# Attention scores on 128 rows everywhere, and a rebalanced weave of routing and expert projection

## The chip, the cores and the metric

The kernel is one program on one core of one Trainium2 chip. The metric is the device time of one execution in microseconds; it was run three times, and the median is 1797.61. One further execution was profiled; it took 1796.13, and every row below comes from it. Times in rows count from the start of its span of 1794.4 us.

## The reference, cut to what matters

256 tokens of width 1024 pass through three blocks in fp32. What the change touches is the scores of the four attentions and the expert layer at the end:

```
# block 1: 'fox' attention (16 heads of 64), then 'nsa' attention (16 heads, 4 key groups)
logits = einsum('bqhd,bkhd->bhqk', q, k) * scale        # fox adds a per-head bias c[q] - c[k]; causal; softmax
# block 2: 8 stick-breaking heads, 8 dilated heads, then a dense feed-forward layer
z  = einsum('bhqd,bhkd->bhqk', q_blk, k) * scale
# block 3: 8 causal heads beside a pooling mixer, then the experts:
q = (h @ w_q).reshape(T, 8, 2, 128);  s = einsum('thpd,hpnd->thpn', q, sub_keys)
sv, si = top_k(s, 16)                                    # 16 of 128 keys in each half
cv, ci = top_k(sv[:, :, 0, :, None] + sv[:, :, 1, None, :], 16)   # 16 of 256 pairs
g = softmax(cv);  expert = si0 * 128 + si1               # 16384 experts
a = gelu(einsum('cd,chkd->chk', x, u_tab[expert]))
y = einsum('chk,chkd->cd', g * a, v_tab[expert])
```

The kernel doesn't gather experts. It computes gelu(x u) for all 16384 of them, multiplies it with a dense matrix of gates (zero where an expert wasn't chosen), and multiplies the product with all of v.

## The kernel before, in words

**Arithmetic.** An fp32 product is made of three products of fp32r halves: `mm3` (L450 to L452) multiplies high by high, low by high and high by low. Every weight tile of 128 x 1024 comes by DMA from the SP queue, ACT copies its high part (`whi`, L241), and DVE subtracts for its low part (`wlo`, L242). For the tiles in the set `W.on_pool` GpSimd (POOL) makes the low part; the set ends ten tiles into the expert matrix u. Three pairs of parts are held, and parts are made two tiles ahead of their use.

**Attention scores.** Head dimension is 64, and two heads lie in the two halves of the 128 partitions. `stack` (L514) builds for a head pair a tile `str` that holds high and low part of one operand in the two halves, a tile `stc` that holds the high part of the other operand twice, and a tile `stl` with its low part, 64 rows for each head. `mm_stack` (L530) then needs two matmuls: one over 128 rows (L533) and one over 64 rows (L534). The second block of 128 queries goes this way. The first block of queries is a plain fp32 matmul over 64 rows (L539 in `attn_scores`, L1114 for the stick-breaking heads), which runs as two passes. The nsa attention has six matmuls for a head, three over 128 rows (L915) and three over 64 (L916).

In each attention stage the heads run as a side of `weave`: the main side is a projection that yields after every step, and after each yield the side's account gets `rate`, and the side runs on until the costs that it yields have used that up:

```
    for _ in main:
        for i, (g, rate) in enumerate(sides):
            acc[i] += rate
            while acc[i] > 0:
                acc[i] -= next(g, 1e9) or 1
    for g, _ in sides:
        drain(g)
```

So rates and yielded costs set the order in which instructions are written; a scheduler then fixes each engine's order at build time. [...]

**The experts.** `peer` first projects the queries (span 925 to 982 us) and finds the top 16 keys on DVE as the heads arrive. Then comes a weave whose main side is the projection by u: 128 tiles of 24 matmuls of 256 columns, made in pairs, with 9 yields to a pair, 576 in all; after a pair ACT applies gelu (L1501). Its only side is `combine`, with the rate `R_PEER`: first `routing` (the last top-16 searches, the softmax of the gates whose exponential is L1453, one-hot expansions of the chosen indices, transposes), which yields 52.5 in all, and then 64 steps of four tokens. A step makes one-hot matrices on DVE (`onehots`, five operations of 512 elements, L1526, L1527 and L1530, cost `OHCOST` = 2.1), multiplies them on PE to a 128 x 128 matrix of gates for a token (12 matmuls, L1549), and multiplies or copies the gates into the activations (L1559 on DVE, L1562 on ACT), cost `EVCOST` = 0.9. Activations of tiles that come later than a step are multiplied with the gates then (L1505). What is left of the side when the main side ends is drained alone. After that come 16 transposes of the residual (L1611) and 16 small ones for a gate vector (L1617), and the projection by v (L1589, 128 tiles, span about 1437 to 1785), for which each tile of the activations is split in two (L1577, L1578).

## Time and profile before

| | |
|---|---|
| three runs, us | 1796.85, 1797.61, 1797.82 (median 1797.61) |
| profiled execution, us | 1796.13 (span 1794.4) |
| PE (TensorE) busy | 1730.8 us, 96% of the span |
| DVE (VectorE) busy | 1291.0 us, 72% |
| ACT (ScalarE) busy | 948.1 us, 53% |
| POOL (GpSimd) busy | 194.9 us, 11% |
| stages in the span, us | fox 0 to 157, nsa to 376, block 2 attention to 527, its feed-forward to 753, block 3 attention to 925, expert queries to 982, u with the weave to 1397, rest of the steps to 1437, v to 1785 |

Rows of a timeline give the start and the duration of an instruction, or of several alike that follow each other (x2), and in brackets how long the engine had been idle and what ended it. PE's matmuls are pipelined, so that the duration of one is longer than the distance to the next: the cost on PE is read from one start to the next. "64*128 64x256" is a matmul over 64 rows with 256 columns. Rows of windows give a stretch, its length, and for PE, its weight loads, DVE, ACT and POOL the busy time and the instructions (x), then TensorE's granted clock as a share of the full 2.4 GHz, the DMA share and GB/s.

### The profile page before, as it was taken

How to read it: one execution, taken by the hardware profiler on the slowest of the kernel's cores; microseconds unless marked ns; L12 is line 12 of the kernel's file. 1: busy time of each engine (PE TensorE's matmuls, PEld its weight loads, DVE VectorE, ACT ScalarE, POOL GpSimd, SP SyncE). 2: the span in 40 equal slices, each digit the busy share in tenths (PEclk: the TensorE clock that was granted, in tenths of full speed). 3: DMA queues.
4: the chain of work that ended last, by engine and by line, in shares of the span. 5: the costliest groups of instructions: out<-in, count | busy, mean ns of one | idle time of the engine just before them, and what ended most of it. 6: DMA issues, size and time to landing. Idle time of an engine off the chain costs nothing.

```text
span 1794.4 us, 31693 instructions
## 1 busy us (share of the span) xinstructions
PE 1730.8 (96%) x12108; PEld 1564.8 (87%) x12108; DVE 1291.0 (72%) x2682; ACT 948.1 (53%) x1783; POOL 194.9 (11%) x194
## 2 busy tenths in 40 slices
PE   8999999999999999999999899999999699999997
PEld 6889897777888999889999799999999588888886
DVE  5777756678767676777667957778889955656565
ACT  5655554555755555566644445544444155555554
POOL 1000124414021000110027300000000000000000
PEclk9999999999999999999999899999999699999999
DMA  6434532248625777534545455545545155655563
GB/s 228 131 120 140 176 110 88 70 168 286 204 95 178 260 259 256 182 123 142 187 156 165 141 188 165 165 154 165 165 154 164 45 179 190 198 190 198 190 197 117
DMA packets 84087, 300.07 MB, mean 167 GB/s; under 512 B 10144, under 2 KB 11040, under 8 KB 83680
## 3 DMA queue, kind: packets, MB, share of 16 engines
q1 hardware_dynamic: 83360, 296.39, 50.1%
q8 instruction: 95, 1.56, 0.4%
q10 hardware_dynamic: 576, 1.66, 0.3%
q14 instruction: 56, 0.46, 0.1%
HBM read 296.04 MB, written 1.05 MB: 166 GB/s over the span
## 4 chain that ended last, share of the span: by engine, by line
PE 81%; DVE 8%; DMA 6%; issue 2%; ACT 2%; POOL 1%; POOLq 0%; SPq 0%; DVEq 0%; ACTq 0%
PE s L1589 10%; PE t L1589 10%; PE pj L450 9%; PE pj L451 9%; PE pj L452 9%; DMA wraw<-in_ada 4%; PE s L450 3%; PE t L450 3%; PE t L452 3%; PE s L451 3%; PE t L451 3%; PE s L452 3%; PE o L1549 2%; PE o L583 2%; DVE wlo L242 1%
## 5 line engine op out<-in xcount | busy, mean ns | idle before, releaser
L242 DVE TENSOR_TENSOR wlo<-wraw,whi 128x1024 fp32r<-128x1024 f32 x480 | 592.2, 1237 | 209.3 <-ACT whi L241 207.7
L241 ACT CAST whi<-wraw 128x1024 fp32r<-128x1024 f32 x504 | 528.3, 1050 | 392.9 <-PE pj L451 131.5
L450 PE MATMUL pj<-hxh,whi 128*128 128x256 f32 x1456 | 423.2, 291 | 4.6 <-ACT vN L1062 1.2
L451 PE MATMUL pj<-hxl,whi 128*128 128x256 f32 x1456 | 413.9, 285 | 0.6 <-DVE hxl L1158 0.4
L452 PE MATMUL pj<-hxh,wlo 128*128 128x256 f32 x1456 | 413.1, 284 | 1.4 <-DVE wlo L242 0.8
L450 PEld LDWEIGHTS pj<-hxh,whi 128*128 128x128 f32 x1456 | 278.3, 191 | 14.2 <-issue 5.0
L452 PEld LDWEIGHTS pj<-hxh,wlo 128*128 128x128 f32 x1456 | 277.7, 191 | 3.6 <-DVE wlo L242 1.2
L451 PEld LDWEIGHTS pj<-hxl,whi 128*128 128x128 f32 x1456 | 278.0, 191 | 2.7 <-DVE hxl L1158 1.1
L1589 PE MATMUL s<-whi,hxl 128*128 128x512 f32 x512 | 158.2, 390 | 0.0
L1589 PE MATMUL t<-whi,hxl 128*128 128x512 f32 x512 | 157.6, 389 | 0.0
L450 PE MATMUL s<-hxh,whi 128*128 128x256 f32 x456 | 131.5, 288 | 1.2 <-DVE st L560 1.2
L1577 ACT CAST hxl<-a 128x256 fp32r<-128x256 f32 x128 | 52.0, 407 | 150.9 <-PE t L1589 150.9
L452 PE MATMUL s<-hxh,wlo 128*128 128x256 f32 x456 | 129.5, 284 | 0.0
L451 PE MATMUL s<-hxl,whi 128*128 128x256 f32 x456 | 129.4, 284 | 0.0
L450 PE MATMUL t<-hxh,whi 128*128 128x256 f32 x424 | 121.9, 288 | 4.7 <-ACT whi L241 4.7
L452 PE MATMUL t<-hxh,wlo 128*128 128x256 f32 x424 | 120.4, 284 | 4.0 <-DVE wlo L242 4.0
L451 PE MATMUL t<-hxl,whi 128*128 128x256 f32 x424 | 120.3, 284 | 0.0
L1589 PEld LDWEIGHTS s<-whi,hxl 128*128 128x128 f32 x512 | 96.3, 188 | 19.9
L1589 PEld LDWEIGHTS t<-whi,hxl 128*128 128x128 f32 x512 | 96.1, 188 | 20.0
L1578 DVE TENSOR_TENSOR hxl<-a,hxl 128x256 fp32r<-128x256 f32 x128 | 54.4, 425 | 64.0 <-PE t L1589 60.0
L291 DVE SCALAR_TENSOR_TENSOR wraw<-wraw,cb 128x1024 f32<-128x1024 f32 x48 | 60.5, 1263 | 44.1 <-DMA wraw<-in_ada 43.9
L450 PEld LDWEIGHTS s<-hxh,whi 128*128 128x128 f32 x456 | 87.6, 192 | 2.2 <-issue 1.9
(400 smaller groups left out, 3422.4 us busy)
## 6 DMA issues: line engine op xcount, KB each, us to landing
wraw<-in_pu SPq DMA_DIRECT2D x128, 512.0 KB
wraw<-in_pv SPq DMA_DIRECT2D x128, 512.0 KB
wraw<-in_b_ffn SPq DMA_DIRECT2D x66, 512.0 KB
wraw<-in_ada SPq DMA_DIRECT2D x48, 512.0 KB
wraw<-in_b_qk SPq DMA_DIRECT2D x24, 512.0 KB
wraw<-in_fox_qk SPq DMA_DIRECT2D x16, 512.0 KB
wraw<-in_b_o SPq DMA_DIRECT2D x16, 512.0 KB
wraw<-in_b_g SPq DMA_DIRECT2D x16, 512.0 KB
```

The lines of the kernel that those rows point to most:

```text
L241: nc.scalar.copy(hi, r)
L242: (nc.gpsimd if self.np in self.on_pool else nc.vector).tensor_tensor(lo, r, hi.bitcast(F32), op=OP.subtract)
L291: nc.vector.scalar_tensor_tensor(t, t, 1.0, cb, op0=OP.mult, op1=OP.mult, accum_out=modT[:, i:i + 1])
L450: nc.tensor.matmul(o, wh, xh, start=start, stop=False)
L451: nc.tensor.matmul(o, wh, xl, start=False, stop=False)
L452: nc.tensor.matmul(o, wl, xh, start=False, stop=stop)
L583: nc.tensor.matmul(o, v(0), pt[:, 0:256], start=start, stop=False)
L1549: nc.tensor.matmul(p[:, t, :], x[:, w[0], :, w[1]], y[i][:, w[0], :, w[1]], start=i == 0 and t == 0, stop=i == 2, skip_group_check=True)
L1577: nc.scalar.copy(ah, src)
L1578: nc.vector.tensor_tensor(al, src, ah.bitcast(F32), op=OP.subtract)
L1589: nc.tensor.matmul(acc[tb][h], x[:, t], w[:, h * 512:h * 512 + 512], start=n == 0 and i == 0, stop=n == P - 1 and i == 2)
```

## The change

1. **Scores.** `stack` makes the stacked operand for both blocks of queries (256 columns instead of 128), and the low part gets its own zero half: the tiles `low` hold 128 rows, of which POOL clears all once, and DVE fills the half of the head. `mm_stack` then runs both matmuls over 128 rows, and the first block of queries uses it too, so that the plain fp32 matmuls L539 and L1114 are gone. In the nsa attention `kl` becomes two tiles with a zero half, and the three matmuls L916 get 128 rows. To make room, the buffers of `qk` are laid out anew (three become one in block 3; in nsa they go into the space of the keys). The matmuls of a score are now L545 (high) and L546 (low), the bias L556.
2. **Weave of the experts.** `R_PEER` goes from 0.36 to 0.43 and `EVCOST` from 0.9 to 1.0; the costs that `routing` yields sum to 37.0 instead of 52.5.
3. **The exponential** of the gates is issued after the first half of the one-hot expansion, not before it.
4. **`W.on_pool`** ends four tiles into u instead of ten: six low parts go from POOL to DVE.
5. A table of 0 to 127 shares a buffer that was there.

From L560 on a line's number after the change differs by some 3 to 12 (the steps' L1526, L1530, L1549, L1559 become L1529, L1533, L1552, L1562; L1453 becomes L1459).

```diff
-R_PEER, TOK, OHCOST, EVCOST = 0.36, 4, 2.1, 0.9
+R_PEER, TOK, OHCOST, EVCOST = 0.43, 4, 2.1, 1.0
-        W.on_pool = set(range(first_u - 14, first_u + 10))
+        W.on_pool = set(range(first_u - 14, first_u + 4))
+        def lows(n, *shape):
+            r = [ph.tile([P, 2, *shape], F32R, name=f"low{i}") for i in range(n)]
+            for t in r:
+                nc.gpsimd.memset(t.bitcast(F32), 0.0)
+            return r
         def stack(rows, cols):
-            r = ph.tile([P, 2, P], F32R, name="str", bufs=SB[i_blk])
+            if low["of"] != i_blk:
+                low.update(of=i_blk, n=lows(SB[i_blk], S))
+            r = ph.tile([P, 2, S], F32R, name="str", bufs=SB[i_blk])
             c = ph.tile([P, 2, S], F32R, name="stc", bufs=SB[i_blk])
-            cl = ph.tile([P, S], F32R, name="stl", bufs=SB[i_blk])
+            cl = low["n"].pop(0)
+            low["n"].append(cl)
...
-                nc.vector.tensor_tensor(cl[a, :], cols[a], c[a, e, :].bitcast(F32), op=OP.subtract)
+                nc.vector.tensor_tensor(cl[a, e, :], cols[a], c[a, e, :].bitcast(F32), op=OP.subtract)
...
-        def mm_stack(o, st, e, stop, skip=False):
-            r, c, cl = st
-            a = HALF[e]
-            nc.tensor.matmul(o, r[:, e, :], c[:, e, :], start=True, stop=False, skip_group_check=skip)
-            nc.tensor.matmul(o, r[a, e, :], cl[a, :], start=False, stop=stop, skip_group_check=skip)
+        def mm_stack(o, st, e, rows, cols, start, stop, skip=False):
+            r, c, cl = (t[:, e, :] for t in st)
+            r = r[:, rows * P:rows * P + P]
+            nc.tensor.matmul(o, r, cols(c), start=start, stop=False, skip_group_check=skip)
+            nc.tensor.matmul(o, r, cols(cl), start=False, stop=stop, skip_group_check=skip)
-        def attn_scores(qT, kT, bias_mm, bias, st2):
+        def attn_scores(bias_mm, bias, st2, e):
             s = ps.tile([P, 512], F32, name="s")
-            nc.tensor.matmul(s[:, 0:P], qT[:, 0:P], kT[:, 0:P], start=True, stop=bias_mm is None)
...
+            for qb in range(2):
+                n = P + P * qb
+                mm_stack(s[:, qb * S:qb * S + S], st2, e, qb, lambda x: x, True, bias_mm is None)
...
-                kl = ph.tile([P, 2, 2, S], F32R, name="kl", tag="Z")
+                kl = [ph.tile([P, 2, 2, S], F32R, name="kl", tag=t) for t in ("Z", "kl")]
...
-                            nc.tensor.matmul(o, qs[c][hs, e, q0:q0 + P], l, start=False, stop=True)
+                            nc.tensor.matmul(o, qs[c][:, e, q0:q0 + P], l, start=False, stop=True)
...
-                yield 6
+                yield 4
...
-                        yield 1.4
+                        yield 1
...
-                nc.scalar.activation(gv, gv, AF.Exp)
-                yield 1.2
+                yield 0.8
                 for tb in range(2):
                     q = eq[tb]
+                    if tb:
+                        nc.scalar.activation(gv, gv, AF.Exp)
...
-                    yield 2.3
+                    yield 1.6
...
-                    yield 2.8
+                    yield 1.8
```

**A head of the fox attention on PE.** Between projection matmuls (L450 to L452) stood, before, the fp32 matmul of the first query block, its bias, and the two matmuls of the second block with their bias (`c_155`, `sel` are the bias operands):

```order
L452 MATMUL pj<-hxh,wlo 128x256
L539 MATMUL s<-qk 128x128
L541 LDWEIGHTS sel
L541 MATMUL s<-c_155,sel 128x128
L533 MATMUL s<-stc,str 128x256
L534 MATMUL s<-stl,str 128x256
L544 LDWEIGHTS sel
L544 MATMUL s<-c_155,sel 128x256
L450 MATMUL pj<-hxh,whi 128x256
```

Now, at a head of the same stage:

```order
L452 MATMUL pj<-hxh,wlo 128x256
L545 MATMUL s<-stc,str 128x256
L546 MATMUL s<-low_478,str 128x256
L556 LDWEIGHTS sel
L556 MATMUL s<-c_155,sel 128x128
L545 MATMUL s<-stc,str 128x256
L546 MATMUL s<-low_478,str 128x256
L556 LDWEIGHTS sel
L556 MATMUL s<-c_155,sel 128x256
L450 MATMUL pj<-hxh,whi 128x256
```

Two matmuls of 256 columns stand in the place of the fp32 one, and the operand with the low part is a `low` tile. Each head of the block 2 dilated heads and of block 3 has the same four matmuls without bias.

**The routing on DVE and ACT, about six tiles of u into the weave.** On DVE, before, these are rows of the top-16 search in the second half of the tokens; no low part (L242) stands among the search's rows:

```order
L1428 TENSOR_TENSOR ra<-ra 128x8x56
L1386 MAX_INDEX ra<-ra 128x8
L1431 TENSOR_TENSOR ra<-ra 128x8x8
L1382 MAX ra<-ra 128x8 x2
L1383 MAX_INDEX ra<-ra 128x8
```

Now, at the same operations (L1430 and L1433 were L1428 and L1431):

```order
L1430 TENSOR_TENSOR ra<-ra 128x8x56
L1387 MAX ra<-ra 128x8
L1433 TENSOR_TENSOR ra<-ra 128x8x8
L242 TENSOR_TENSOR wlo<-wraw,whi 128x1024
L1388 MAX_INDEX ra<-ra 128x8
L1384 MAX ra<-ra 128x8 x2
```

A low part now stands between two searches. From the search's start to the last multiplication of the routing there are 16 of them on DVE, where 9 were, all of them behind the search. On ACT, before, the exponential (L1453) stood behind the gelus of the third pair of u, a high part ahead of the next pair's gelus:

```order
L1501 ACTIVATE a_10601<-t 128x256 x2
L241 CAST whi<-wraw 128x1024
L1453 ACT_TABLE_LOAD
L1453 ACTIVATE ra<-ra 128x256
L241 CAST whi<-wraw 128x1024
L1501 ACT_TABLE_LOAD
L1501 ACTIVATE a_10601<-pj 128x256 x2
```

Now it (L1459) stands behind the fifth pair's:

```order
L1504 ACTIVATE a_10637<-pj 128x256 x2
L241 CAST whi<-wraw 128x1024 x2
L1504 ACTIVATE a_10637<-s 128x256 x2
L1459 ACT_TABLE_LOAD
L1459 ACTIVATE ra<-ra 128x256
L241 CAST whi<-wraw 128x1024 x2
L1504 ACT_TABLE_LOAD
L1504 ACTIVATE a_10637<-t 128x256 x2
```

It has moved by two pairs of u.

**The end of the weave on PE.** Before, the last row of the last step stands long behind the last projection matmul and directly ahead of the transposes and of the projection by v (L1589):

```order
L1549 MATMUL o<-ohy_17326,ohx 128x128
L1611 MATMUL o<-ident,xT 128x128 x12
L1589 MATMUL s<-whi,hxl 128x512 x2
L1611 MATMUL o<-ident,xT 128x128 x4
L1589 MATMUL s<-wlo,hxl 128x512 x2
```

Now (L1614, L1620 and L1592 were L1611, L1617 and L1589) the last projection matmul stands there:

```order
L450 MATMUL pj<-hxh,whi 128x256
L451 MATMUL pj<-hxl,whi 128x256
L452 MATMUL pj<-hxh,wlo 128x256
L1614 MATMUL o<-ident,xT 128x128 x8
L1620 MATMUL pj<-ident,modT 128x128 x8
L1614 MATMUL o<-ident,xT 128x128 x8
L1592 MATMUL s<-whi,hxl 128x512 x2
```

All 64 steps stand ahead of it; before, 51 did, and 13 stood behind it.

## Rows read from the trace of the kernel before

**Rows 1.** The page: the engines' busy time, share of the span and instructions.

```profile
PE 1730.8 (96%) x12108; PEld 1564.8 (87%) x12108; DVE 1291.0 (72%) x2682; ACT 948.1 (53%) x1783; POOL 194.9 (11%) x194
```

**Rows 2.** The timeline of PE at a head of the fox attention.

```profile
81.46 0.28 PE L452 MATMUL pj<-hxh,wlo 128*128 128x256 f32 x1
81.67 0.48 PE L539 MATMUL s<-qk 64*128 64x128 f32 x2
...
82.13 0.36 PE L533 MATMUL s<-stc,str 128*128 128x256 f32 x1
82.42 0.38 PE L534 MATMUL s<-stl,str 64*128 64x256 f32 x1
82.73 0.28 PE L544 MATMUL s<-c,sel 128*128 128x256 bf16 x1
82.77 0.37 PE L450 MATMUL pj<-hxh,whi 128*128 128x256 f32 x1
```

**Rows 3.** The timeline of PE at a head of the nsa attention.

```profile
322.54 0.28 PE L915 MATMUL s<-k,q 128*128 128x256 f32 x1
322.75 0.39 PE L916 MATMUL s<-kl,q 64*128 64x256 f32 x1
323.06 0.39 PE L915 MATMUL s<-k,q 128*128 128x256 f32 x1
...
324.32 0.39 PE L452 MATMUL pj<-hxh,wlo 128*128 128x256 f32 x1
```

**Rows 4.** The timeline of PE around a dilated head of block 2: the last projection matmul ahead of it and the first behind it.

```profile
497.38 0.28 PE L452 MATMUL pj<-hxh,wlo 128*128 128x256 f32 x1
...
498.63 0.39 PE L450 MATMUL pj<-hxh,whi 128*128 128x256 f32 x1
```

**Rows 5.** The timeline of PE at the start of block 3's heads, where the fp32 matmuls of two heads stand one behind the other.

```profile
787.07 0.49 PE L539 MATMUL s<-qk 64*128 64x128 f32 x4 [0.86 <-DVE qk L626]
787.49 0.39 PE L452 MATMUL pj<-hxh,wlo 128*128 128x256 f32 x1
```

**Rows 6.** Windows (columns as above) within the nsa, the fox, the block 2 and the block 3 attention.

```profile
288.00:302.00 14.00, 14.00 (x81) 10.84 (x81) 10.41 (x56) 10.63 (x39) 5.94 (x12) 1.00 0.01 2
45.00:150.00 105.00, 105.00 (x756) 90.58 (x755) 78.26 (x200) 64.46 (x154) 5.17 (x4) 1.00 0.38 121
430.00:530.00 100.00, 99.37 (x640) 80.42 (x641) 74.30 (x159) 71.23 (x170) 11.76 (x19) 1.00 0.49 160
790.00:825.00 35.00, 34.03 (x222) 27.63 (x222) 28.51 (x82) 22.19 (x59) 2.78 (x3) 1.00 0.32 101
```

**Rows 7.** The instructions of line 523 (the copy into the stacked operand) in the whole span: shortest, median and longest in ns, first and last start.

```profile
L523 ACT CAST str<-qk x40: 281/295/299, 49.0 to 815.7; 64x128 fp32r<-64x128 f32 x40
```

**Rows 8.** Windows of the weave by u: its start with the routing, its last 97 us, and the steps that follow it.

```profile
981.60:1021.20 39.60, 30.98 (x242) 30.48 (x242) 38.62 (x182) 17.90 (x25) 18.57 (x8) 0.87 0.37 120
1300.00:1397.30 97.30, 97.30 (x907) 96.57 (x906) 89.30 (x172) 43.53 (x107) 0.00 (x0) 1.00 0.50 160
1397.30:1437.00 39.70, 25.42 (x189) 18.67 (x187) 37.41 (x88) 5.71 (x12) 0.00 (x0) 0.62 0.09 27
```

**Rows 9.** The timelines of ACT and, below it, of PE where the exponential of the routing stands.

```profile
1011.56 0.42 ACT L1453 ACTIVATE ra<-ra 128x256 f32<-128x256 f32 x1 [9.57 <-DVE ra L1452]
1012.97 0.58 PE L450 MATMUL t<-hxh,whi 128*128 128x256 f32 x1 [4.65 <-ACT whi L241]
1017.73 0.58 PE L452 MATMUL t<-hxh,wlo 128*128 128x256 f32 x1 [3.97 <-DVE wlo L242]
```

**Rows 10.** Timelines of POOL (the first row) and DVE in the routing; the last row groups DVE's low parts from 1011.12 to 1037.6, where the routing ends.

```profile
986.37 2.41 POOL L242 TENSOR_TENSOR wlo<-wraw,whi 128x1024 fp32r<-128x1024 f32 x1 [0.48 <-ACT whi L241]
982.39 0.49 DVE L1382 MAX8 ra<-ra 128x8 f32<-128x128 f32 x2 [0.93 <-ACT ra L1402]
986.62 2.31 DVE L1427 TENSOR_TENSOR ra<-ra 128x128 f32<-128x128 f32 x1
1000.04 0.41 DVE L1427 TENSOR_TENSOR ra<-ra 128x128 f32<-128x128 f32 x1
1001.27 2.19 DVE L1431 TENSOR_TENSOR ra<-ra 128x64 f32<-128x64 f32 x1
L242 DVE TENSOR_TENSOR wlo<-wraw,whi 128x1024 fp32r<-128x1024 f32 x9 | 10.8, 1218 | 0.0
```

**Rows 11.** The timeline of PE at a step late in the weave.

```profile
1331.20 0.28 PE L451 MATMUL t<-hxl,whi 128*128 128x256 f32 x1
1331.32 0.28 PE L452 MATMUL t<-hxh,wlo 128*128 128x256 f32 x1
1331.45 0.86 PE L1549 MATMUL o<-ohy,ohx 128*128 128x128 bf16 x12
1332.12 0.36 PE L450 MATMUL pj<-hxh,whi 128*128 128x256 f32 x1
1332.32 0.28 PE L451 MATMUL pj<-hxl,whi 128*128 128x256 f32 x1
```

**Rows 12.** The timeline of PE in the steps behind the weave: the first of them, one wait from the middle, and the first transposes behind the last.

```profile
1397.19 1.55 PE L1549 MATMUL o<-ohy,ohx 128*128 128x128 bf16 x24
...
1419.73 1.22 PE L1549 MATMUL o<-ohy,ohx 128*128 128x128 bf16 x10 [0.67 <-DVE ohy L1530]
...
1432.34 1.05 PE L1611 MATMUL o<-ident,xT 128*128 128x128 f32 x4
```

More of the change, by code (lines that the diff above doesn't have):

```diff
@@ L525, in stack @@
                 nc.vector.tensor_tensor(r[b, e, :], rows[a], r[a, e, :].bitcast(F32), op=OP.subtract)
-                nc.vector.tensor_tensor(cl[a, :], cols[a], c[a, e, :].bitcast(F32), op=OP.subtract)
+                nc.vector.tensor_tensor(cl[a, e, :], cols[a], c[a, e, :].bitcast(F32), op=OP.subtract)
                 nc.scalar.copy(c[b, e, :], cols[a])
             return r, c, cl
-        def mm_stack(o, st, e, stop, skip=False):
-            r, c, cl = st
-            a = HALF[e]
-            nc.tensor.matmul(o, r[:, e, :], c[:, e, :], start=True, stop=False, skip_group_check=skip)
-            nc.tensor.matmul(o, r[a, e, :], cl[a, :], start=False, stop=stop, skip_group_check=skip)
-        def attn_scores(qT, kT, bias_mm, bias, st2):
-            s = ps.tile([P, 512], F32, name="s")
-            nc.tensor.matmul(s[:, 0:P], qT[:, 0:P], kT[:, 0:P], start=True, stop=bias_mm is None)
-            if bias_mm is not None:
-                nc.tensor.matmul(s[:, 0:P], bias_mm[0], bias_mm[1][:, 0:P], start=False, stop=True)
-            mm_stack(s[:, P:P + S], *st2, bias_mm is None)
-            if bias_mm is not None:
-                nc.tensor.matmul(s[:, P:P + S], bias_mm[0], bias_mm[1], start=False, stop=True)
-            return softmax((s[:, 0:P], s[:, P:P + S]), bias)
+        def mm_stack(o, st, e, rows, cols, start, stop, skip=False):
[4 more added lines that the diff above has]
+        def attn_scores(bias_mm, bias, st2, e):
+            s = ps.tile([P, 512], F32, name="s")
+            for qb in range(2):
+                n = P + P * qb
+                mm_stack(s[:, qb * S:qb * S + S], st2, e, qb, lambda x: x, True, bias_mm is None)
+                if bias_mm is not None:
+                    nc.tensor.matmul(s[:, qb * S:qb * S + n], bias_mm[0], bias_mm[1][:, 0:n], start=False, stop=True)
+            return softmax((s[:, 0:P], s[:, S:2 * S]), bias)
         def softmax(s, bias):
@@ L689, in qk_evac @@
                 nc.vector.tensor_tensor(qk[:, c0 // 2], p, rqk, op=OP.mult)
-                stacks[c0 // 2] = stack(qk[:, c0 // 2, 0, P:], qk[:, c0 // 2, 1, :])
+                stacks[c0 // 2] = stack(qk[:, c0 // 2, 0, :], qk[:, c0 // 2, 1, :])
                 cnt["qk"] = c0 // 2 + 1
@@ L880, in q_evac @@
                 nc.vector.tensor_tensor(x, p, rq[:, None, :].to_broadcast([P, 2, S]), op=OP.mult)
-                qT[c0 // 2] = q = ph.tile([P, 2, S], F32, name="qk", bufs=2)
+                qT[c0 // 2] = q = ks[2][:, c0 // 2 % 2]
                 rope([(q, (slice(None),) * 3)], x, C["ropeC"][:, None, :].to_broadcast([P, 2, S]),
@@ L1069, in qk_evac @@
                 q, k = qk[:, c, 0, :], qk[:, c, 1, :]
-                stacks[c] = stack(k[:, :P], q) if c < 4 else stack(q[:, P:], k)
+                stacks[c] = stack(k, q) if c < 4 else stack(q, k)
                 cnt["qk2"] = c + 1
@@ L1103, in attn @@
                         c = h // 2
[L1104 removed]
                         while cnt.get("qk2", 0) <= c:
                             yield
[L1107 removed]
                         if h < 8:
                             z = ps.tile([P, 512], F32, name="s")
[L1110 to L1115 removed]
+                            for kb, cols_of in enumerate((lambda x: x, lambda x: x[:, None, P:].to_broadcast([P, 2, P]))):
+                                o = kb * S
+                                mm_stack(z[:, o:o + S], stacks[c], h % 2, kb, cols_of, kb == 0, False, True)
                                 nc.tensor.matmul(z[:, o:o + P], sbm[:, 0, :], sbm[:, 1, :], start=False, stop=kb == 1,
@@ L1238, in qk_evac @@
                 nc.scalar.copy(x, p)
-                qk[c] = ph.tile([P, 2, S], F32, name="qk", bufs=3)
+                qk[c] = ph.tile([P, 2, S], F32, name="qk", bufs=1)
                 rope([(qk[c], (slice(None),) * 3)], x, rt[:, 0], rt[:, 1], space)
-                stacks[c] = stack(qk[c][:, 0, P:], qk[c][:, 1, :])
+                stacks[c] = stack(qk[c][:, 0, :], qk[c][:, 1, :])
                 cnt["qk3"] = c + 1
@@ L1358, in peer @@
             nc.scalar.dma_start(sk, A["sk"])
-            iota = ph.tile([P, P], F32, name="iota")
+            iota = take("a", P)
             nc.scalar.dma_start(iota, A["iota"])
```

40 lines of the change are left out of this document (14 added, 26 removed).

## The prediction, made before the changed kernel ran

> **What bounds the kernel now.** I read the page first, then windows of the stages, then PE's timeline at the places that change. PE is busy for 96% of the span [rows 1], in most windows at a granted clock of 1.00, that is 2.4 GHz [rows 6], so time is saved where PE's own work gets shorter, or where it stands still or at a lower clock. The windows show which it is where. In the fox, block 2 and block 3 attentions PE is busy for 105.00 of 105, 99.37 of 100 and 34.03 of 35 us, with DVE at 75 to 81% [rows 6]: work removed from PE there shortens the stage as long as DVE and the softmax behind it keep up. In the weave by u there are two soft spots [rows 8]: its start, where PE is busy for only 30.98 of 39.6 us at a clock of 0.87, and the stretch behind it, 25.42 of 39.70 us at 0.62. There DVE is the busy engine (38.62 and 37.41 us).
>
> **The scores.** The step from one projection matmul to the next is 0.12 us (1331.20 to 1331.32) [rows 11]. A fox head takes 81.58 (0.12 behind the start at 81.46) to 82.77, 1.19 us [rows 2]. Of that a 256-column matmul over 128 rows that is followed by one over 64 rows takes 0.29 (82.13 to 82.42), and the 64-row one 0.31 (82.42 to 82.73), each some 2.5 times the 0.12: what is dear is going from 128 rows to 64 and back. Without that the head is four matmuls of 0.12, two biases of 0.04 (82.73 to 82.77), and some allowance for the change between bf16 and fp32r at each bias, 0.07 as an estimate (behind the bf16 matmuls of a step the next one takes 0.20 and not 0.12, 1332.12 to 1332.32 [rows 11]); 0.70 us, with bounds of 0.60 and 0.88. Saved: 16 heads by 0.49 = 7.8 us. A dilated head or one of block 3 takes 1.13 (497.50 to 498.63) [rows 4] and becomes 0.48: 16 by 0.65 = 10.4. For the 8 stick-breaking heads, with two bias matmuls of the larger kind, I estimate 0.46 each, 3.7. An nsa head is six matmuls in 1.78 (322.54 to 324.32), with 0.21 and 0.31 in turn [rows 3], and becomes 0.72: 16 by 1.06 = 17.0. Gross 38.9 us.
>
> How much is kept depends on the covers. In the fox stage DVE has 78 us of work in 105 [rows 6], so 8 us less PE time still leaves it under 82%; I keep 7 of 7.8 (bounds 5 and 9.5). For blocks 2 and 3 I keep 12 of 14.1 (9 to 15). In nsa the window shows PE 14.00, DVE 10.41, ACT 10.63 and POOL 5.94 of 14 us [rows 6]: in itself room, but with a score's two banks refilled head by head, the chain score, softmax, exponential, POOL's normalization, transposes is nearly as long as PE's work beside it. When a head's scores shrink by 1.06 us, PE will come early to the next transposes and wait. I keep 10 of 17 (5 to 17).
>
> The price is wider stack copies: 40 on ACT, now 0.295 us for 128 columns [rows 7]; 256 columns took ACT 0.42 in the exponential [rows 9], so 0.125 more each, and as many on DVE. That is 5 us on either engine, in stages where ACT is busy for 61 to 71% and DVE for 75 to 81% [rows 6]; I cost it at nothing, and if the cover were gone it would be those 5 us. POOL's clearing stands on an engine with 5 to 12 us of work in these windows. The first query block now waits for the stack, where it waited for `qk` alone (0.86 us once [rows 5]): minus 1. Attention in sum: 7 + 12 + 10 - 1 = 28 us (17 to 40).
>
> Here a rule speaks against the change. In rows 5 four 64-row matmuls of two heads, which lie in different halves of the rows, take only 0.42 us (787.07 to 787.49), so a pair overlapped. The Trainium skill ("TensorE: Matmul & The Clock Gate", section "Why this matters for your kernels") says that small matmuls in distinct row groups run concurrently and that a single one over few rows takes as long as one over all 128. By it a 64-row matmul would cost what a 128-row one does, the gain from rows would be nil, and an overlap would be thrown away. The trace agrees with the overlap at that one place; it doesn't agree with equal cost where rows alternate (0.31 against 0.12 [rows 2, 11]). The Trainium skill's page "TensorEngine Tiling (Array Packing)", section "Key Properties", says that a change of the tiling mode drains TensorE, which fits that 0.31.
>
> **The weave by u.** First the stretch behind it. The steps that were left run from 1397.19 to 1432.34, 35.1 us, 24 matmuls to begin with for two steps [rows 12]; 11 more follow, 13 in all. In the weave a step costs PE 0.67 + 0.08 = 0.745 us (1331.45 to 1332.12, and then 0.20 to the next one instead of 0.12) [rows 11]. The account shows why they fit now: routing took 52.5 / 0.36 = 146 of the 576 yields, and 430 yields x 0.36 / 3.0 gives 51 steps; now 37 / 0.43 = 86 and 490 x 0.43 / 3.1 = 68, more than the 64 there are. So 35.1 go and 13 x 0.745 = 9.7 come. The 16 transposes that stood between those steps now wait behind the weave: minus 1. The other transposes, the copies and the split before the projection by v stay as they are.
>
> Second its start. ACT sits 9.57 us at the exponential for DVE's routing (till 1011.56), and the high part that PE needs stands behind it; PE then waits 4.65 us for that and 3.97 for a low part [rows 9], with matmuls at 1.2 GHz after it: 39.6 - 30.98 = 8.6 idle and about 1.5 of slow matmuls, 10 us. Now the exponential stands two pairs later, 11.5 us of PE. DVE's routing took from 982.39 to 1037.57, 55.2 us, with 9 low parts of 1.14 in it, 10.3 [rows 10]. It also had operations that took 2.31 and 2.19 us beside low parts on POOL (986.37), where the same operation took 0.41 at 1000.04; three such, 5.7 us. They go, since POOL's last low part now ends before 986. That leaves 39.2 us, and with 16 low parts (18.3) it ends at 982.4 + 57.5 = 1039.9. PE, undisturbed, comes to the routing's transposes behind 19.6 tiles of 24 x 0.12 = 2.88 us, at 1038.1. So PE waits about 2 us there (0 to 8) in place of 10: 8 won.
>
> Third, the price: DVE. In the last 97.3 us it is busy for 89.30 [rows 8]. A step took 3.0 / 0.36 = 8.33 yields, 1.85 tiles, 1.85 x 2.88 + 0.745 = 6.08 us of PE; so 16 steps stand there, with 5.58 us of DVE each, 2.1 of it low parts. Now a step comes every 7.2 yields, 1.61 tiles: PE 5.38, DVE 1.61 x 1.14 + 3.47 = 5.30. DVE is at 98.6% late in the weave; it was 92%. I take 3 us of waits (0 to 15).
>
> In sum: 35.1 - 9.7 - 1 + 8 - 3 = 29 us (17 to 32).
>
> **Sum.** 28 + 29 = 57. The profiled execution took 1796.13 us, so 1739; the median of the runs lies 1.5 above it, so **1741 us**.
>
> **Rivals.** *The softmax chain eats the scores' gain.* For: nsa's tight chain. Against: the full PE and the free DVE of the others [rows 6]. With 2 us kept in nsa and 10 elsewhere: 1796 - 12 - 29 + 1.5 = 1757. *DVE becomes the bound late in the weave.* For: 98.6%. If it is late by 0.5 us in each of the last 30 steps, 15 us go: about 1755. *A padded matmul gains nothing* (the rule above): only the weave's 29 are left, 1769; rows 2 and 3 speak against it. *Slower.* If DVE's demand passes PE's 5.38 us, PE waits in each step, as it did behind the weave (0.67 us ahead of ten matmuls [rows 12], clock 0.62 [rows 8]), and its clock falls. At 1.2 GHz a step is 38.6 matmuls of some 0.21 and 1.1, 9.3 us; then DVE catches up and the clock returns. At half and half 7.4, 2.0 us more than 5.38; over 30 steps 60, more than the 57 won: about 1801. It decides from 5.38 us of DVE per step, 0.08 from my estimate; against it, PE showed no wait worth naming in that window with DVE at 92%.
>
> **Numbers.** My forecast 0.65, with a range of its own of 1726 to 1756; softmax chain 0.14; DVE late 0.11; nothing from rows 0.05; slower 0.04, and 0.01 for a cancellation near zero. The range of 1725 to 1766 leaves out the last three and tails of the first. 0.2% (3.6 us) is about what a measurement of this kernel can tell from no change: faster 0.95, same 0.01, slower 0.04.
>
> **What would show it.** Right: fox heads near 0.7 us and nsa heads near 0.72 on PE; no 64-row score matmul left; attention stages ending some 6, 16 and 28 us earlier by fox, nsa and block 3; one wait of a few us near tile 20 of u; the projection by v starting within 6 us of the last projection matmul by u. Wrong: waits of PE for `pn` or for ACT in nsa, one-hot matmuls that wait for `ohy` in the last 100 us of the weave, or a clock below 1.00 there.

## The result, and the profile after

The changed kernel takes 1725.9 us (median of four runs, 1724.79 to 1728.64), against 1797.23 before in the same comparison: a ratio of 0.9615, interval 0.9598 to 0.9631. That is 71 us less, where 57 were forecast; the time lies just inside the range, at its lower end. The profiled execution took 1728.64 us, 67.5 less than the profiled one before. PE's line of the page, against [rows 1]:

```profile
PE 1680.3 (97%) x12108; PEld 1545.8 (90%) x12108; DVE 1294.4 (75%) x2691; ACT 959.2 (56%) x1813; POOL 185.7 (11%) x198
```

PE's busy time fell by 50.5 us and its idle time by 17, so the gain is mostly work or slow matmuls taken from PE, not waits. The stages show where. In each I took the start of the same projection matmul (the L450 with the same number in PE's order) in both traces:

| place | before | after | gain so far |
|---|---|---|---|
| end of the fox stage (L450 no. 240) | 166.2 | 158.8 | 7.4 |
| end of nsa (no. 520) | 391.4 | 362.8 | 28.6 |
| start of the feed-forward of block 2 (no. 720) | 548.3 | 513.0 | 35.3 |
| behind it (no. 1040) | 723.3 | 690.5 | 32.7 |
| behind block 3's attention (no. 1440) | 930.8 | 894.2 | 36.6 |
| last projection by u (no. 2575) | 1396.8 | 1365.1 | 31.8 |
| last matmul of the projection by v | 1784.9 | 1717.5 | 67.5 |

The heads have shrunk as computed. A fox head on PE, against [rows 2]:

```profile
87.08 0.28 PE L452 MATMUL pj<-hxh,wlo 128*128 128x256 f32 x1
87.20 0.28 PE L545 MATMUL s<-stc,str 128*128 128x256 f32 x1
87.31 0.28 PE L546 MATMUL s<-low,str 128*128 128x256 f32 x1
...
87.80 0.28 PE L556 MATMUL s<-c,sel 128*128 128x256 bf16 x1
87.84 0.36 PE L450 MATMUL pj<-hxh,whi 128*128 128x256 f32 x1
```

From 87.20 to 87.84 it is 0.64 us; it was 1.19. The second matmul now starts 0.11 behind the first, where 0.29 stood. An nsa head, against [rows 3]:

```profile
235.31 0.28 PE L923 MATMUL s<-k,q 128*128 128x256 f32 x1
235.42 0.28 PE L924 MATMUL s<-kl,q 128*128 128x256 f32 x1
...
236.01 0.40 PE L832 MATMUL o<-whi,zh 128*128 128x256 f32 x1
```

It takes 0.70 (235.31 to 236.01) instead of 1.78.

Windows of the kernel before: the nsa stage, and 40 us in it where its heads begin.

```profile
157.00:376.00 219.00, 210.88 (x1343) 181.74 (x1342) 148.20 (x406) 118.19 (x268) 59.50 (x79) 0.97 0.34 112
225.00:265.00 40.00, 40.00 (x194) 35.69 (x194) 21.22 (x70) 20.23 (x47) 7.21 (x11) 0.91 0.35 121
```

The same of the kernel after, and below them the start of the weave by u and 100 us late in it, against [rows 8] (busy us of PE, PE's loads, DVE, ACT, POOL; then the clock):

```profile
150.00:348.00 198.00, 188.49 (x1344) 171.40 (x1342) 150.09 (x406) 117.09 (x267) 59.67 (x80) 1.00 0.38 124
225.00:265.00 40.00, 37.85 (x253) 35.19 (x253) 29.49 (x97) 24.45 (x60) 17.75 (x19) 1.00 0.37 123
945.20:984.80 39.60, 38.78 (x315) 37.84 (x314) 39.35 (x190) 21.30 (x30) 2.64 (x2) 1.00 0.47 158
1200.00:1300.00 100.00, 100.00 (x947) 99.18 (x946) 93.32 (x188) 47.24 (x108) 0.00 (x0) 1.00 0.47 159
```

The nsa stage is 198 us long, and was 219. PE's idle time in it is 9.5 us and was 8.1. The clock is 1.00 and was 0.97. At the start of the weave PE is busy for 38.78 of 39.6 us, where it was 30.98, at a clock of 1.00 instead of 0.87. What is left of PE's waits there, by the timeline (the two longest):

```profile
995.76 0.39 PE L452 MATMUL t<-hxh,wlo 128*128 128x256 f32 x1 [0.54 <-DVE wlo L242]
1004.73 0.44 PE L1480 MATMUL o<-ident,ra 128*128 128x128 f32 x2 [1.55 <-DVE ra L1469]
```

And the end of the weave, against [rows 12]:

```profile
1365.31 0.28 PE L452 MATMUL pj<-hxh,wlo 128*128 128x256 f32 x1
1365.43 1.04 PE L1614 MATMUL o<-ident,xT 128*128 128x128 f32 x8
1366.31 1.95 PE L1620 MATMUL pj<-ident,modT 128*128 128x128 f32 x16
1368.43 1.15 PE L1614 MATMUL o<-ident,xT 128*128 128x128 f32 x8 [0.17 <-ACT hxh L1615]
1369.33 0.48 PE L1592 MATMUL s<-whi,hxl 128*128 128x512 f32 x1
```

From the last projection matmul at 1365.31 to the first of the projection by v it is 4.0 us; in [rows 12] the 13 steps alone were 35.1.

### The profile page after: what moved, and what is told of

Its sections match the earlier page's. It is cut to its first block, busy times and chain, and to the rows that moved or that the text cites. A ratio compares the mean times of both kernels' runs of the same rounds, so it can differ in the third digit from the quotient of the medians.

```text
span 1726.9 us, 31770 instructions
## 1 busy us (share of the span) xinstructions
PE 1680.3 (97%) x12108; PEld 1545.8 (90%) x12108; DVE 1294.4 (75%) x2691; ACT 959.2 (56%) x1813; POOL 185.7 (11%) x198
## 4 chain that ended last, share of the span: by engine, by line
PE 52%; DVE 3%; ACT 1%; issue 0%; POOLq 0%; POOL 0%; DVEq 0%; ACTq 0%
PE s L1592 10%; PE t L1592 10%; PE pj L450 5%; PE pj L451 5%; PE pj L452 5%; PE o L1552 3%; PE s L450 2%; PE t L450 2%; PE s L452 2%; PE s L451 2%; PE t L451 2%; PE t L452 2%; DVE wlo L242 1%; PE s L1401 0%; PE o L595 0%
## 5 line engine op out<-in xcount | busy, mean ns | idle before, releaser
L242 DVE TENSOR_TENSOR wlo<-wraw,whi 128x1024 fp32r<-128x1024 f32 x486 | 601.9, 1241 | 194.1 <-ACT whi L241 192.3
L450 PE MATMUL pj<-hxh,whi 128*128 128x256 f32 x1456 | 422.8, 291 | 5.7 <-ACT vN L1070 1.9
L452 PE MATMUL pj<-hxh,wlo 128*128 128x256 f32 x1456 | 412.3, 284 | 1.9 <-DVE wlo L242 1.4
L450 PEld LDWEIGHTS pj<-hxh,whi 128*128 128x128 f32 x1456 | 278.2, 191 | 14.0 <-issue 4.8
L452 PEld LDWEIGHTS pj<-hxh,wlo 128*128 128x128 f32 x1456 | 277.5, 191 | 3.8 <-DVE wlo L242 2.2
L1592 PE MATMUL s<-whi,hxl 128*128 128x512 f32 x512 | 157.8, 389 | 0.0
L1592 PE MATMUL t<-whi,hxl 128*128 128x512 f32 x512 | 157.6, 389 | 0.0
L450 PE MATMUL s<-hxh,whi 128*128 128x256 f32 x456 | 130.9, 287 | 1.7 <-DVE st L572 1.7
L452 PE MATMUL s<-hxh,wlo 128*128 128x256 f32 x456 | 129.3, 283 | 0.4 <-DVE wlo L242 0.4
L450 PE MATMUL t<-hxh,whi 128*128 128x256 f32 x424 | 121.4, 286 | 0.0
L452 PE MATMUL t<-hxh,wlo 128*128 128x256 f32 x424 | 119.7, 282 | 0.9 <-DVE wlo L242 0.8
L1592 PEld LDWEIGHTS t<-whi,hxl 128*128 128x128 f32 x512 | 96.1, 188 | 19.9
L1592 PEld LDWEIGHTS s<-whi,hxl 128*128 128x128 f32 x512 | 95.9, 188 | 20.0 <-ACT hxl L1580 0.2
L450 PEld LDWEIGHTS s<-hxh,whi 128*128 128x128 f32 x456 | 87.0, 191 | 2.3 <-issue 2.3
L452 PEld LDWEIGHTS s<-hxh,wlo 128*128 128x128 f32 x456 | 86.9, 191 | 1.1 <-DVE wlo L242 0.8
```

Source lines behind the costliest of these rows:

```text
L242: (nc.gpsimd if self.np in self.on_pool else nc.vector).tensor_tensor(lo, r, hi.bitcast(F32), op=OP.subtract)
L450: nc.tensor.matmul(o, wh, xh, start=start, stop=False)
L452: nc.tensor.matmul(o, wl, xh, start=False, stop=stop)
L1592: nc.tensor.matmul(acc[tb][h], x[:, t], w[:, h * 512:h * 512 + 512], start=n == 0 and i == 0, stop=n == P - 1 and i == 2)
```

## The experiments

Medians with their range, and the ratio to the kernel before with its 95% interval. The kernel before ran beside each set; its medians were 1794.93, 1794.08, 1794.41 and 1793.45. Its runs scatter from 1787 to 1802, more than any of the others; places in the traces are compared below where the times can't tell.

| run | us | ratio |
|---|---|---|
| e1_scores_only | 1757.17 (1756.27 to 1759.53) | 0.9793 [0.9756, 0.983] |
| e2_weave_only | 1761.62 (1758.21 to 1764.55) | 0.9821 [0.9784, 0.9859] |
| e3_rows64 | 1766.43 (1765.89 to 1769.13) | 0.9847 [0.981, 0.9884] |
| e4_nsa64 | 1741.73 (1740.15 to 1744.41) | 0.971 [0.9673, 0.9747] |
| e5_pool10 | 1730.99 (1727.13 to 1736.86) | 0.9651 [0.9614, 0.9688] |
| e9_before_pool4 | 1785.94 (1782.34 to 1792.08) | 0.9959 [0.994, 0.9978] |
| e7_steps51 | 1753.59 (1748.07 to 1755.1) | 0.9765 [0.9732, 0.9797] |
| e8_steps_fast | 1734.63 (1733.54 to 1739.54) | 0.9677 [0.9645, 0.9709] |
| e11_pool10_keep | 1732.46 (1728.96 to 1733.97) | 0.9651 [0.9633, 0.967] |
| e10_routing46 | 1722.59 (1718.34 to 1724.89) | 0.9599 [0.9579, 0.9619] |
| e12_both | 1733.02 (1728.88 to 1735.3) | 0.9657 [0.9637, 0.9677] |
| e13_pool_every_other | 1727.62 (1725.64 to 1731.59) | 0.9622 [0.9598, 0.9645] |

### The two halves apart

**Scores alone.** The changed kernel with the numbers, costs, set and line of the weave put back:

```diff
-R_PEER, TOK, OHCOST, EVCOST = 0.43, 4, 2.1, 1.0
+R_PEER, TOK, OHCOST, EVCOST = 0.36, 4, 2.1, 0.9
-        W.on_pool = set(range(first_u - 14, first_u + 4))
+        W.on_pool = set(range(first_u - 14, first_u + 10))
...
```

> The kernel before with the new scores alone; weave, exponential and the set of POOL's tiles as before. Theory A (each attention keeps all that its matmuls save, and in the nsa stage three stretches of 1.2 GHz go as well): the projection by expert queries starts 36 to 39 us earlier, time 1758 to 1762. Theory B (the softmax chain takes back half of nsa's gain, as the prediction had it): 1769. Theory C (the gain is one of both parts together, since the weave's timing hangs on when the attention ends): neither part alone gives its share, time above 1775.

It took 1757.17, under even theory A's range. By the trace the projection of the expert queries starts 38.3 us earlier than before, and nothing is gained or lost behind it (38.6 at the end). Theory B, which was the prediction's, fails.

**The weave alone.** The kernel before with those edits.

> The kernel before with the weave alone (rate, costs, exponential, POOL's tiles); scores as before. The parts add up: the attention's times as before, the weave and what follows 31 us shorter, time 1766, and the changes of this kernel and of the one with scores alone sum to that of the whole change. Theory C: time above 1775.

1761.62, 4 us under the forecast. By the trace (of the fastest of its four executions, 1758.21) it is 30.8 us shorter from the expert queries on: its lead on the kernel before grows from 7.15 us to 37.95. The 7 us ahead of them lie in attention stages that were not edited; about half of it is the clock: 20.4 us at 1.2 GHz ahead of 376 us in the trace of the kernel before, 13.6 in this one, worth 3.4; the rest is spread over these stages and its cause stays open. The ratios multiply: 0.9793 x 0.9821 = 0.9618, against 0.9615 for the whole change. The halves don't interact; theory C fails.

### Rows, or the fp32 matmuls that are gone

**All second matmuls on 64 rows.** Stacks and everything else as changed:

```diff
-            nc.tensor.matmul(o, r, cols(cl), start=False, stop=stop, skip_group_check=skip)
+            a = HALF[e]
+            nc.tensor.matmul(o, r[a], cols(cl)[a], start=False, stop=stop, skip_group_check=skip)
...
-                            nc.tensor.matmul(o, qs[c][:, e, q0:q0 + P], l, start=False, stop=True)
+                            nc.tensor.matmul(o, qs[c][hs, e, q0:q0 + P], l[hs], start=False, stop=True)
```

> The changed kernel, but the second matmul of every score multiplies only the 64 rows that are not zero (in all four attentions); stacks, buffers, number and order of the matmuls stay as changed. If going between 128 and 64 rows is what costs: 0.36 us for each such matmul outside nsa (two a head: 40 heads by 0.72 = 29 us) and 17 in nsa, with the three stretches of 1.2 GHz back in nsa (7 us): 46 to 53 us slower than the changed kernel, 1772 to 1779. If a 64-row matmul costs the same as a 128-row one and the gain came from the fp32 matmuls that are gone: as the changed kernel, 1726.

40 us slower than the changed kernel (1766.43 against 1725.9), so rows are what costs. The forecast of 46 to 53 was too high: a fox head takes 1.21 us in the rows below (89.18 to 90.39, the start of the next projection matmul), 0.57 more than in the changed kernel, where 0.72 were put; and the nsa stage is 19.6 us longer than there, where 24 were put. PE's timeline of a fox head in it (L547 is the second matmul):

```profile
89.18 0.28 PE L545 MATMUL s<-stc,str 128*128 128x256 f32 x1
89.39 0.38 PE L547 MATMUL s<-low,str 64*128 64x256 f32 x1
89.70 0.23 PE L557 MATMUL s<-c,sel 128*128 128x128 bf16 x1
89.74 0.36 PE L545 MATMUL s<-stc,str 128*128 128x256 f32 x1
90.04 0.38 PE L547 MATMUL s<-low,str 64*128 64x256 f32 x1
90.35 0.28 PE L557 MATMUL s<-c,sel 128*128 128x256 bf16 x1
```

L545 and L547 start 0.21, 0.31, 0.04 (behind the bias), 0.30 and 0.31 apart in place of 0.11 to 0.21. The fp32 matmuls are gone in this kernel too, and its fox stage is as long as before (its lead on the changed kernel is -7.5 us at the end of that stage, and the kernel before has -7.4). So the gain is that of rows that no longer change between matmuls. Both sides of a change are dear, the 128-row matmul ahead of a 64-row one (0.21 and 0.30) as well as the 64-row one (0.31); but no run has two 64-row matmuls of 256 columns directly behind each other, so the price of the change isn't separated from that of a 64-row matmul as such.

**nsa alone on 64 rows** (the second edit only).

> The changed kernel, but the three second matmuls of an nsa head multiply 64 rows only. Theory A: nsa's rows were worth 17 us of matmul time and 7 of clock, 17 to 24 us slower than the changed kernel: 1743 to 1750, with stretches of 1.2 GHz in nsa. Theory B (the chain is nearly as long as PE's work): 10 us slower, 1736. Another rival: nsa gained from the new places of q and k, not from rows: 1726 to 1728.

1741.73, 15.8 us slower than the changed kernel, just under theory A's 17 to 24. In the traces the nsa stage ends 17.9 us later (L450 no. 520), at the lower end of that range; theory B's 10 and the other rival's 0 are out. Windows as above, of this kernel:

```profile
150.00:366.00 216.00, 207.90 (x1343) 178.96 (x1342) 147.87 (x406) 118.14 (x267) 60.67 (x80) 0.98 0.35 113
225.00:265.00 40.00, 40.00 (x219) 34.44 (x218) 23.99 (x83) 22.59 (x56) 12.44 (x15) 0.91 0.30 96
```

The clock of 0.91 in the 40 us where the heads begin is that of the kernel before. A stretch of 6.8 us at 1.2 GHz stands there (238.9 to 245.7), worth 3.4 us; the matmuls themselves account for the other 14.5, of a gross 17.

### What had stalled the start of the weave

**Ten tiles on POOL** in the changed kernel:

```diff
-        W.on_pool = set(range(first_u - 14, first_u + 4))
+        W.on_pool = set(range(first_u - 14, first_u + 10))
```

> The changed kernel, but POOL makes the low parts of the first ten tiles of u again. The exponential then stands behind the third pair's gelus on ACT, although its line is the changed one. Theory A (where the exponential stands on ACT is what stalls PE, and the set of POOL's tiles decides it): PE waits for a high part behind the exponential again, 8 to 9 us with matmuls at 1.2 GHz after it, 7 to 10 us slower than the changed kernel in that stretch, about 1734. Theory B (the smaller costs in routing and the later line removed the stall): no stall, 1724 to 1727.

1730.99, 5 us slower, and by the trace the weave is 5.3 us longer. That is less than theory A's 7 to 10, since the short waits of the changed kernel are gone, but the stall is back: ACT's wait at the exponential, and below it PE's two waits, are those of [rows 9] almost to the digit:

```profile
972.72 0.42 ACT L1459 ACTIVATE ra<-ra 128x256 f32<-128x256 f32 x1 [9.57 <-DVE ra L1454]
974.13 0.58 PE L450 MATMUL t<-hxh,whi 128*128 128x256 f32 x1 [4.65 <-ACT whi L241]
978.76 0.58 PE L452 MATMUL t<-hxh,wlo 128*128 128x256 f32 x1 [3.84 <-DVE wlo L242]
```

Thus neither the smaller costs nor the changed line removes the stall: with ten tiles on POOL, the scheduler puts the exponential behind the third pair wherever the line stands. In the other direction the line does nothing either: with the old line and four tiles (the next run) ACT's rows stand in the same order as in the changed kernel, the exponential behind the fifth pair, and DVE's low parts stand between the searches as there, some of them a few rows earlier or later.

**Four tiles on POOL** in the kernel before, the same edit the other way round.

> The kernel before with one number changed: POOL's set ends at the fourth tile of u. The exponential then stands behind the fifth pair's gelus, without its line or a cost being changed. Theory A: the stall of 8.6 us at the start of the weave shrinks to 1 to 4, 6 to 9 us faster than before in that stretch, all else as before: about 1789. Theory B: no change in that stretch or a longer one, since DVE has six low parts more: 1797 to 1800.

```profile
981.60:1021.20 39.60, 38.71 (x316) 37.90 (x316) 38.84 (x189) 21.61 (x30) 2.81 (x2) 1.00 0.47 157
```

That window was 30.98 us busy at 0.87 in [rows 8]; by the trace 7.4 us are won, and the time is 8 lower. One number of the diff did all that the change won at the start of the weave.

**Ten tiles, but the exponential late.** To tell the exponential from the set, it is held in program order:

```diff
-                        nc.scalar.activation(gv, gv, AF.Exp)
+                        tc.keep_in_program_order(nc.scalar.activation(gv, gv, AF.Exp))
```

> The changed kernel with ten tiles of u on POOL, as in the run before, but the exponential kept in program order, so that it stands behind the seventh pair's gelus on ACT instead of the third's. Theory A (the place of the exponential alone makes the stall): the waits of 4.65 and 3.84 us are gone, and DVE has six low parts less, so the small waits for low parts go too: the weave 2 to 3 us shorter than in the changed kernel, 1723 to 1726. Theory B (POOL's low parts beside DVE's searches make the stall, by the 2 us operations): the stall of 8 us stays, 1731.

1732.46: no faster than with the early exponential. The exponential no longer waits (it stands at 997.99), and yet PE stands still once for 9.06 us, by DVE's timeline and, in the last two rows, PE's:

```profile
976.15 2.29 DVE L1460 TENSOR_TENSOR ra<-ra 128x4096 bf16<-128x4096 bf16 x1
978.36 1.22 DVE L242 TENSOR_TENSOR wlo<-wraw,whi 128x1024 fp32r<-128x1024 f32 x1
970.29 0.28 PE L451 MATMUL t<-hxl,whi 128*128 128x256 f32 x1
979.63 0.58 PE L452 MATMUL t<-hxh,wlo 128*128 128x256 f32 x1 [9.06 <-DVE wlo L242]
```

Theory A fails here, and with it the prediction's reason for the stall. PE has the high part and waits for a low part of DVE, the first that DVE makes for u (tile 10). In DVE's queue it stands behind all searches and the first expansion (L1460). With four tiles on POOL DVE's low parts stand between the searches. The wait at the exponential was a part of the same 9 us. Theory B's forecast (the stall stays, 1731) came true, and the trace shows its share. From the start of the weave to L1460 DVE runs the same 197 operations (low parts left out) in both kernels; they keep it busy for 35.4 us here and for 29.4 in the changed kernel. Three of them, which run beside POOL's low parts (the first two rows), make the difference:

```profile
948.39 5.30 POOL L242 TENSOR_TENSOR wlo<-wraw,whi 128x1024 fp32r<-128x1024 f32 x2 [0.48 <-ACT whi L241]
962.79 2.62 POOL L242 TENSOR_TENSOR wlo<-wraw,whi 128x1024 fp32r<-128x1024 f32 x1 [0.48 <-ACT whi L241]
949.23 2.19 DVE L1433 TENSOR_TENSOR ra<-ra 128x64 f32<-128x64 f32 x1
951.34 3.58 DVE L1426 CAST ra<-ra 128x512 bf16<-128x512 uint32 x1
963.28 2.21 DVE L1433 TENSOR_TENSOR ra<-ra 128x64 f32<-128x64 f32 x1
```

The same three in the changed kernel:

```profile
951.93 1.34 DVE L1426 CAST ra<-ra 128x512 bf16<-128x512 uint32 x1
952.87 0.46 DVE L1433 TENSOR_TENSOR ra<-ra 128x64 f32<-128x64 f32 x1
964.47 0.20 DVE L1433 TENSOR_TENSOR ra<-ra 128x64 f32<-128x64 f32 x1
```

So of the wait of 9 us about 6 come from searches that are slower beside POOL and about 3 from the low part's place behind them: an estimate from these two sums, as no run has the one without the other.

**Routing's costs at 46 instead of 37**, all 64 steps still in the weave:

```diff
-                yield 4
+                yield 5
...
-                        yield 1
+                        yield 1.25
-                yield 1.7
+                yield 2.1
...
```

> The changed kernel with the costs that routing yields raised from 37 to 46, so that the first step stands some four tiles later and DVE's routing work is thinner among the low parts; all 64 steps still fit. If the waits of PE in the changed kernel's routing (0.2 us at each of six low parts, 0.5, and 1.55 at the transposes) come from DVE having more than PE's time for a tile: 2 to 3 us shorter weave, 1723 to 1726. If they come from latency alone, as the changed kernel.

1722.59. In the trace the weave is 2.3 us shorter than in the changed kernel: the waits of 0.54 and 1.55 us are down to 0.2 and gone, those of about 0.2 stayed. It is the fastest version measured. By the intervals (0.9599 and 0.9615) it can't be told from the changed kernel; only the trace tells.

**Both edits** (ten tiles with the late exponential, and costs of 46).

> Both of the other two edits of this call: ten tiles on POOL, the exponential kept in program order, routing costs of 46. No wait of PE above 0.3 us left in routing: 3 us shorter weave than the changed kernel, 1722 to 1726; a third engine's wait in their place would show as the changed kernel's time or above.

1733.02, with the same single wait of 9.06 us. The expectation fell with theory A.

**POOL makes tiles 0 to 3, 5, 7 and 9** (with costs of 46), so that DVE's low parts still stand between the searches, but fewer:

```diff
-        W.on_pool = set(range(first_u - 14, first_u + 4))
+        W.on_pool = set(range(first_u - 14, first_u + 4)) | {first_u + 5, first_u + 7, first_u + 9}
```

> The kernel with routing costs of 46, and POOL makes the low parts of tiles 5, 7 and 9 of u in addition to the first four, so that DVE has three low parts less in the searches, but still has some standing between them. Theory Q (the stall with ten tiles on POOL comes from DVE's first own low part, which stands behind all searches in its queue while PE needs it before): no wait of 4 us or more; the weave as with routing costs of 46 alone or up to 1 us shorter, 1722 to 1724. If POOL's work beside DVE's searches made the stall: part of it returns, 3 us or more, 1726 and above.

The wait of 9 us is gone, but shorter ones are back, all for DVE's low parts; PE's two longest:

```profile
964.19 0.39 PE L452 MATMUL pj<-hxh,wlo 128*128 128x256 f32 x1 [1.46 <-DVE wlo L242]
971.66 0.39 PE L452 MATMUL s<-hxh,wlo 128*128 128x256 f32 x1 [1.46 <-DVE wlo L242]
```

In sum PE's waits there are 4.8 us, and the weave is 3.2 us longer than with costs of 46 alone. So theory Q's forecast holds for the long wait and not for the time; the rival's (3 us or more, 1726 and above) is met. DVE is slower beside POOL here too: this row takes 0.33 us with costs of 46 alone, and the 197 operations take 31.1 us, where they take 29.5.

```profile
955.25 2.38 DVE L1429 TENSOR_TENSOR ra<-ra 128x128 f32<-128x128 f32 x1
```

The run thus doesn't decide between the place in the queue and POOL's work; by e11's trace both count. Which of them makes the two waits of 1.46 us (the place in the queue, the row above, or the low parts of 1.61 and 1.78 us that ran beside POOL's, where 1.2 is usual) stays open.

### The steps

**13 steps behind the weave again**, in the changed kernel:

```diff
-R_PEER, TOK, OHCOST, EVCOST = 0.43, 4, 2.1, 1.0
+R_PEER, TOK, OHCOST, EVCOST = 0.43, 4, 2.1, 2.0
```

> The changed kernel with EVCOST 2.0 instead of 1.0: routing as it is, but 13 of the 64 steps stand behind the last projection matmul again. By the prediction's sum they take 35 us there, and the 13 x 0.745 us go from the weave, and 1 for the transposes: 24 us slower than the changed kernel, about 1750, with a clock of about 0.6 in that stretch. If the stretch was costly for another reason (what comes with the end of the weave, not the steps), 0 to 10 us slower.

1753.59, 28 us slower; by the trace 26 (the end of the projection by v, with 0.4 taken off that were there ahead of the weave). The stretch behind the weave is that of [rows 8]:

```profile
1356.10:1396.10 40.00, 25.78 (x192) 18.98 (x190) 37.61 (x88) 5.83 (x12) 0.00 (x0) 0.62 0.09 27
```

So it is the place of the steps that costs. In the weave the 13 steps that are missing save 9.6 us, which the prediction had at 9.7.

**A step every 3.9 yields** instead of 7.2, so that DVE can't keep up:

```diff
-R_PEER, TOK, OHCOST, EVCOST = 0.43, 4, 2.1, 1.0
+R_PEER, TOK, OHCOST, EVCOST = 0.43, 4, 1.1, 0.57
```

> The changed kernel with OHCOST 1.1 and EVCOST 0.57: a step every 3.9 yields instead of 7.2, routing as it is. PE has 0.86 x 2.88 + 0.745 = 3.23 us for a step, DVE 0.86 x 1.14 + 1.68 for the one-hot matrices + 0.7 to 1.3 for the gates, 3.4 to 4.0, so DVE is the bound in the steps, by 0.2 to 0.8 us each; the steps end halfway through the weave and PE is alone with projections after that. Theory A (the prediction's slower rival: from there on PE waits in each step and its clock falls): 64 x 0.5 = 32 us and more, 1755 to 1775, a clock below 1.00 in the steps. Theory B (three pairs of parts and two sets of one-hot matrices let PE run ahead; the work is the same in sum): 1726 to 1735.

1734.63, 9 us slower; by the trace the weave is 12.4 us longer. Windows of the steps and of the stretch behind them:

```profile
1010.00:1186.00 176.00, 170.32 (x1700) 166.44 (x1700) 173.01 (x405) 95.05 (x236) 0.00 (x0) 1.00 0.41 133
1186.00:1370.00 184.00, 181.95 (x1556) 180.52 (x1555) 114.61 (x182) 85.74 (x140) 0.00 (x0) 1.00 0.53 174
```

DVE is busy for 173 of 176 us and is the bound. PE still doesn't stand still for long (170.32 busy), and the clock is 1.00 throughout. The price is in the steps: from the projection matmul ahead of each to the second behind it, beyond two ordinary 0.12, the sum over all steps is about 61 us, and 48.5 in the changed kernel. Theory A, the clock's fall, fails; theory B's time holds.

## Why the prediction was right, and where it was off

The attention stages gained 36.6 us (L450 no. 1440), where 28 were forecast, and the weave with what follows it 30.9, where 29 were. So the mechanism and the places of the gains were right. The time lies inside the range by 1 us only; in the profiled pair 67.5 us were gained instead of 57, and nsa's term alone is 11 over its forecast, while the other errors nearly cancel.

**What a change of rows costs** was right, the centre of the forecast. A fox head was put at 0.70 and takes 0.64, an nsa head at 0.72 and takes 0.70, and e3 shows that the 64 rows, not the fp32 passes, were dear. The rule of the Trainium skill by which a single matmul over few rows takes as long as one over 128 ("TensorE: Matmul & The Clock Gate", "Why this matters for your kernels") would have left the changed kernel's time in e3; it became 40 us longer.

**How much is kept.** Fox kept 7.4 (forecast 7). Blocks 2 and 3 kept 6.7 and 3.9, together 10.6 (forecast 12). The step that failed is "I keep 10 of 17" in nsa: it gained 21 us, beyond its upper bound. The chain of scores, softmax, exponential and transposes was said to take back half; PE's idle time in the stage rose by only 1.4 us. That a chain is nearly as long as the work beside it in one window was not a measurement of what happens when that work shrinks; e4 gives 14.5 of 17. And the sum had no term for the clock: the profile before had three stretches in nsa at 1.2 GHz, 13.6 us long and so worth 6.8, the one after none. 14.5 + 6.8 is the 21, in this pair of executions. The stretches stood in the trace before, and the sum left them out.

**Feed-forward.** Not in the forecast: 2.5 us were lost there in the profiled execution, with 6.8 us at 1.2 GHz from 641.6 behind a wait of 1.8 us for an activation. The change doesn't force it: e8 and e12 have the same feed-forward without such a stretch. But of the nine profiled kernels whose nsa heads have 128 rows throughout, six have one of 3.4 or 6.8 us that begins there, between 640.9 and 646.7 us, behind a wait of 1.0 to 1.8 us at L1172, and of the other five none has. Whether the change makes it likelier stays open.

**The end of the weave.** Forecast 35.1 off, 9.7 into the weave, 1 for transposes. Behind the last projection matmul 35.7 us went, and e7 confirms the sum of the three by 26 against 24.

**The start** was forecast at 8 us and gave less, for another reason than the one given. From the first to the last L450 the weave by u got 4.9 us longer (418.4 to 423.3). With 9.7 for steps that leaves 4.8 won at the start. Read from one start to the next beyond 0.12, PE's waits and slow matmuls there cost 9.6 us before (10 were put) and 4.7 after, where 2 were allowed. The 2 came from a wrong start: the prediction lets PE begin the weave at 981.6, where the window of [rows 8] begins, but its first projection matmul by u is this one, 3.1 us earlier:

```profile
978.47 0.28 PE L450 MATMUL pj<-hxh,whi 128*128 128x256 f32 x1
```

With it PE comes to the transposes at 1034.9 and not at 1038.1, and the same sum gives a wait of 5.0. Not the exponential stood in the way, as I read from [rows 9], but the first low part behind the searches in DVE's queue, and the searches were slowed by POOL (e11). The 5.7 us that the prediction counted for operations slowed by POOL come near the 6.0 of e11's trace. The number that mattered was that of POOL's tiles (e9).

**DVE late in the weave** was allowed 3 us and cost none. At 1200 to 1300 us DVE is busy for 93.32 of 100 with 18.6 steps of 5.38 us in it, 5.0 for a step and not 5.30: the work per step that is no low part was carried over from the kernel before, and it is smaller in this window, which lies earlier among the tiles of u: a step's gates are multiplied on DVE only with tiles that are already made (L1562, 21.4 us for 18.6 steps; its L1559 before took 22.1 us for 16 in the window of [rows 8]). The rule for the slower rival was wrong as well: in e8 DVE was the bound and the clock stayed at 1.00. So -9.7 + 8 - 3 = -4.7 met the measured -4.9 by two errors that cancel.

Of the rivals, "the softmax chain eats the gain" is refuted by e1 and e4 (e1 gains 38.3 us of the gross 38.9), "a padded matmul gains nothing" by e3, the clock's fall by e8, and "DVE late" by the late window.

## What to carry to other kernels

Where matmuls over few rows stand among matmuls over all rows, price them from the trace, one start to the next, before thinking of columns: here a matmul over 128 rows, half of them zeros, took 0.12 us among its like, and one over the 64 rows that count 0.31. When PE waits for one of two parts, look for the first instruction of the late engine in its queue, for what stands ahead of it and for how much longer that takes beside another engine's work, and not for the wait that happens to be the longest. And give stretches of lower clock in the profile of before a term of their own in the sum, with both ends, since they may or may not come back.

## What the runs showed of the hardware that I had not expected

Stretches at 1.2 GHz come and go between executions of the same matmuls: the unedited attention stages of e2 had 6.8 us less of them than those of the kernel before. In nsa there is a pattern. In the five profiled kernels whose nsa heads alternate between 128 and 64 rows (before, e2, e3, e4, e9) a stretch of 6.8 or 10.2 us begins between 238.9 and 247.9 us, among the first heads. In the nine with 128 rows throughout none begins there; eight of them have one of 3.4 us at 262 to 265 or at 333 to 337, or both. Summed over nsa (157 to 376 us) the five have 6.8 to 13.6 us, 10.2 in the mean, the nine 0 to 6.8, 4.9 in the mean. So of the 6.8 us that the clock gave in the profiled pair less than half is to be expected in another execution ((10.2 - 4.9) / 2 = 2.7). What links heads and clock was not tested further.
